# A two-layer decoder trunk: the order of four PSUM banks in the down projection, the PSUM tile of two projection tiles, and the step of two transposes are changed

## The chip, the cores and the metric

The kernel runs on one core of one Trainium2 chip. The metric is the device time of one execution in microseconds (us), lower is better. Three runs of the kernel before took 2271.39, 2271.67 and 2273.57 us, with a median of 2271.67 us.

## The reference

The model has two layers over 1024 tokens of width 1024, in float32. Layer 0 mixes tokens by multi-head latent attention, layer 1 by differential attention (two causal softmax maps per head, whose difference weights the values). After each mixer comes a dense MLP with squared ReLU, and every sub-layer is followed by a residual and a layer norm:

```python
for i in range(2):
    m = mla(x, ...) if i == 0 else diff_attn(x, ...)
    x = layernorm(alpha * x + m)
    x = layernorm(alpha * x + square(relu(x @ w_up)) @ w_down)   # 1024 -> 4096 -> 1024
```

`diff_attn` starts with `x @ w_qkv`, which gives queries, keys and values of 8 heads. The change touches the end of the MLP (the product with `w_down`, the residual and the layer norm) and the first head of `x @ w_qkv` in layer 1.

## The kernel before, in words

All products are made in two float16 halves, so one mathematical product is three matmuls: high by high, high by low, low by high (`mm3`, L186).

**PSUM.** The eight banks are shared by three kinds of tile, two of each: `ps_wide`, 128x1024 float32, which is a pair of banks; `ps_tp`, one bank; `ps_mm`, one bank. The score tiles `ds` of the attention are `ps_wide` tiles, the query/key/value tiles `qkv` are `ps_mm` tiles, and transposes land in `ps_tp`.

**The down projection** (`mixer_out_and_ffn`, once for layer 0 with names ending in A, once for layer 1 ending in B) is done as a fast 2x2 block scheme with seven block products, m = 0 to 6, each summed over NS = 8 steps `st`. A set of four banks, `banks[0..3]`, holds the sums of four token tiles of 128. Sets are taken alternately from two `ps_tp` and two `ps_mm` tiles, and from two `ps_wide` tiles. The last set, that of m = 6, is of `ps_wide` tiles, `w[0]` and `w[1]`: `banks[0]` and `banks[1]` are the halves of `w[0]`, `banks[2]` and `banks[3]` those of `w[1]`. In a step, 24 matmuls write `yA` (or `yB`), six to each bank (`products`). ACT and DVE prepare the operands `h16`, `w16` of the step three later (`d_operands`, L265 and L266). At the end of a set DVE adds the four banks to the rows X2 (`add_y`, L1251).

**The tail.** The last four steps of m = 6 are held back and done bank by bank: for i = 0 to 3, 24 matmuls finish `banks[i]` (called products(i) here), DVE adds it to two rows (add(i)), and the layer norm of row tile 4+i follows: a mean (L1265), a sum of squares on ACT (L1270), a reciprocal root (L160 to L165, over ACT and DVE) and, one i later, the application (L248, L251, called apply(4+i) here) with its store to DRAM on SP's queue.

**The next x.** In layer 0 the finished rows are also transposed for layer 1 (`to_xt`, 8 transposes on PE at L217, two scalings on ACT, two subtractions on DVE). Tiles 0 and 1 are transposed during m = 5, tiles 2 and 3 in the steps (6, 1) and (6, 2), tiles 4 and 5 between the groups of the tail, tiles 6 and 7 after it. On ACT the step (6, 1) and (6, 2) also has squares of the weights of `qkv` (`at`).

**The start of layer 1.** `qkv_part` makes the `qkv` tiles of head 0 for token tiles 0 to 3 first, 24 matmuls each, needing only transposed tiles 0 to 3. Each is then read out by ACT and DVE (`qkv_out`, L1543 to L1546), which frees its PSUM bank. The attention follows, with the later `qkv` tiles as filler between its scores and value products.

**What sets the order.** Inside `with in_order():` each engine keeps the written order. The MLP is one such block, the first four `qkv` tiles are another; between blocks, and in the whole attention, the order on each engine is made when the program is built, by a planner that runs through a simulated timeline (`schedule_with_timeline_sim=True`). On the chip each engine then works through its queue in that order.

Of the kernel before, what the change touches and what calls it, by code (L numbers as in the profile page):

```python
# [72 lines left out]
def trunk(ctx: ExitStack, tc: tile.TileContext, a: dict, inv_freq: bass.AP, out: bass.AP):  # L73
# [16 lines left out]
    def ps_wide(name):  # L90
        return ps.tile([P, 1024], F32, tag="s", name=name)

    def ps_tp(name):
        return ps.tile([P, 512], F32, tag="tp", name=name)

    def ps_mm(name):
        return ps.tile([P, 512], F32, tag="mm", name=name)
# [92 lines left out]
    def p3(lh, ll, rh, rl):  # L190
        return [(lh, rh), (lh, rl), (ll, rh)]
# [16 lines left out]
    def new_xt16(c, nm):  # L208

        return [xtp.tile([P, 2, 4, 512], F16, tag="xt", name=f"xt_{nm}{c}{hf}") for hf in range(2)]  # L210

    def transpose_in16(src, xt_c, ii, nm, scale, tile_of=None):
        for hf in range(2):
            pt = (tile_of or ps_tp)(f"tp_{nm}{hf}")[:, :512].rearrange("p (k q) -> p k q", k=4)
            for k in range(4):
                kk = hf * 4 + k
                nc.tensor.transpose(out=pt[:, k, :], in_=src[:, kk * P : (kk + 1) * P], identity=ident)  # L217
            tk = slice(ii * P, (ii + 1) * P)
            scaled_split(xt_c[hf][:, 0, :, tk], xt_c[hf][:, 1, :, tk], pt, scale)
# [688 lines left out]
    def mixer_out_and_ffn(layer, pa, pb, o_steps, st, n_early, ffn_dst, nm, at={}):  # L908


        with ExitStack() as fs:
# [25 lines left out]
            def up_load(g):  # L937
                raws[g] = tuple(slot(pb, [P, 2, 4, P], F32, f"wu{nm}{g}_r{n}") for n in range(2))
                for f_ in range(2):
                    nc.sync.dma_start(  # L940
                        out=raws[g][f_].rearrange("p z k n -> p (z k) n"), in_=wu[:, :, f_, g, :]
                    )
# [23 lines left out]
            def up_cast(g):  # L966
                raws[g] += (total_in(raws[g][4], f"wu{nm}{g}"),)
# [194 lines left out]
            xt_n = [None, None]  # L1162
# [63 lines left out]
            def bank_set(wide, tag):  # L1226
                if wide:
                    w = [ps_wide(f"y{nm}{tag}{n}") for n in range(2)]
                    return [t[:, hf * 512 : (hf + 1) * 512] for t in w for hf in range(2)]
                return [ps_tp(f"y{nm}{tag}{n}") for n in range(2)] + [ps_mm(f"y{nm}{tag}{n}") for n in range(2)]  # L1230

            def products(dst, i, op, first, last):
# [23 lines left out]
            def to_xt(dst, i, w, tile_of=None):  # L1256
                if i % 4 == 0:
                    dst[i // 4] = new_xt16(i // 4, f"{w}{nm}")
                transpose_in16(X[i], dst[i // 4], i % 4, f"{w}{nm}{i}", sx[:, 2:3], tile_of)
# [33 lines left out]
            for n, i in enumerate(order):  # L1293
# [31 lines left out]
                else:  # L1325
# [4 lines left out]
                    t = x_sums(i - 4, nc.gpsimd if n < NT - 1 else nc.vector)  # L1330
# [10 lines left out]
            with in_order():  # L1341
                for g in range(NG):
                    w = g + 2 < NG
                    if g + 3 < NG:
                        up_load(g + 3)
                    if g + 1 < NG:
                        wd_fetch(g + 1)
                    if w:
                        up_cast(g + 2)
                    if g == NG - 2:  # L1350
                        down_sum(NA, "A")
                    if 0 < g < NG - 1:
                        u_p1(g + 1)
                    u_p7(g)
                    if w:
                        up_scale(g + 2)
                        up_split(g + 2, 0)
                    if g + 1 < NG:
                        u_p6(g + 1)
                    if w:  # L1360
                        up_split(g + 2, 1)
                    if g == NG - 2:
                        down_scale(NA, "A")
                    u_p4(g)
                    if w:
                        up_split(g + 2, 2)
                    if g + 3 < NG:
                        up_sq(g + 3)
                        up_add(g + 3)
                    if g >= NG - 2:  # L1370
                        d_operands(*next(ready))
                    u_p3(g)
                    if w:
                        up_split(g + 2, 3)
                    if g + 1 < NG:
                        if g > 0:
                            u_p2(g + 1)
                        u_p5(g + 1)
                        wd_scan(g + 1)
                    u_out(g)  # L1380
                    if g == NG - 3:
                        for _ in range(3):
                            d_load(*next(loaded))
                d_load(*next(loaded))
                d_operands(*next(ready))

                load_gb("ffn", "f")
                tail, sets = [], 0
                for m, st_ in steps:
                    nxt_ = next(loaded, None)  # L1390
                    if nxt_:
                        d_load(*nxt_)
                    if (m, st_) == (0, 1):
                        for i in range(NT):
                            X[i] = row(f"X2{nm}{i}")
                            nc.sync.dma_start(out=X[i], in_=x2_d[layer, i * P : (i + 1) * P, :])
                    first = st_ == 0 or (m == 0 and st_ == NS - 1)
                    last = st_ == NS - 1 or (m == 0 and st_ == NS - 2)
                    if first:
                        sets += 1  # L1400
                        banks = bank_set(sets % 2 == 0, f"{m}{st_}")
                    late = m == 6 and st_ >= NS - 4
                    if late:
                        tail.append((m, st_))
                    else:
                        for i in range(4):
                            products(banks[i], i, ops[m, st_], first, last)
                        ops.pop((m, st_))
                    if (m, st_) == (0, 0):
                        down_sum(NS, "B")  # L1410
                    if (m, st_) == (0, 2):
                        down_scale(NS, "B")
                    nxt_ = next(ready, None)
                    if nxt_:
                        d_operands(*nxt_)
                    if last and not late:
                        for i in range(4):
                            add_y(banks[i], i, m, "A" if m == 0 and not first else "B")
                    if m == 5:
                        i = st_ // 2  # L1420
                        if st_ % 2 == 0:
                            fin_stats(i)
                        else:
                            if layer == 0 and i in (1, 2):
                                to_xt(xt_n, i - 1, "n", ps_wide)
                            fin_rstd(i)
                            fin_apply(i)
                    if m == 6 and st_ in (1, 2) and layer == 0:
                        to_xt(xt_n, 1 + st_, "n")
                    for step in at.get((m, st_), ()):  # L1430
                        step()
                for i in range(4):
                    for n, key in enumerate(tail):
                        products(banks[i], i, ops[key], False, n == 3)
                    if layer == 0 and i > 1:
                        to_xt(xt_n, 2 + i, "n")
                    add_y(banks[i], i, 6, "B")
                    fin_stats(4 + i)
                    if i > 0:
                        fin_apply(3 + i)  # L1440
                    fin_rstd(4 + i)
                if layer == 0:
                    to_xt(xt_n, 6, "n")
                fin_apply(7)
                if layer == 0:
                    to_xt(xt_n, 7, "n")
# [67 lines left out]
    with ExitStack() as df:  # L1514
# [9 lines left out]
        qkT, dv, dpts, qkv_ps, qk_t, pe1 = {}, {}, {}, {}, {}, {}  # L1524

        def qkv_part(h, i, k0):
            if k0 == 0:
                qkv_ps[h, i] = ps_mm(f"qkv{h}_{i}")[:, :384]
            pq = qkv_ps[h, i]
            for k in (k0, k0 + 1):  # L1530
                xt_ = xt1[i // 4][k // 4]
                xh, xl = (xt_[:, w, k % 4, i % 4 * P : (i % 4 + 1) * P] for w in range(2))
                wh, wl = (w16[h][k // 2][:, w, k % 2 * 384 : (k % 2 + 1) * 384] for w in range(2))
                mm3(pq, p3(xh, xl, wh, wl), first=k == 0, last=k == KT - 1)
            if k0 + 2 == KT:
                qkv_out(h, i, qkv_ps.pop((h, i)))
# [205 lines left out]
```

## Time and profile before

| | |
|---|---|
| median of three runs | 2271.67 us |
| profiled execution, its own time | 2272.7 us |
| its span in the trace | 2270.9 us |
| time around the span | 1.8 us |
| mean granted TensorE clock | 0.972 |
| DVE busy | 1678.9 us (74%) |
| ACT busy | 1279.8 us (56%) |

PE is TensorE's matmuls, PEld its weight loads, DVE VectorE, ACT ScalarE, POOL GpSimd, SP the queue from which the transfers are issued. Times in the trace are from the start of the span. In a timeline a row is a run of like instructions on one engine: start, duration, engine, line, operation, output and inputs, shape and count. A bracket at the end is the time for which the engine sat idle before it, and what ended that. The last granted clock of a window is a share of 2.4 GHz, so 0.50 is 1.2 GHz.

The stages that matter here lie as follows: the down projection of layer 0 from 791.8 us (the first `yA` matmul) to its tail at 1077 to 1128 us, the differential attention after it up to about 1600 us, and the down projection of layer 1 from 1964.1 us to the end.

### The profile page before, as it was taken

How to read it: one execution, taken by the hardware profiler on the slowest of the kernel's cores; microseconds unless marked ns; L12 is line 12 of the kernel's file. 1: busy time of each engine (PE TensorE's matmuls, PEld its weight loads, DVE VectorE, ACT ScalarE, POOL GpSimd, SP SyncE). 2: the span in 40 equal slices, each digit the busy share in tenths (PEclk: the TensorE clock that was granted, in tenths of full speed). 3: DMA queues.
4: the chain of work that ended last, by engine and by line, in shares of the span. 5: the costliest groups of instructions: out<-in, count | busy, mean ns of one | idle time of the engine just before them, and what ended most of it. 6: DMA issues, size and time to landing. Idle time of an engine off the chain costs nothing. (4 is left out here: it accounts for less than half of the span.)

```text
span 2270.9 us, 31756 instructions
## 1 busy us (share of the span) xinstructions
PE 2127.6 (94%) x11255; PEld 1189.7 (52%) x11255; DVE 1678.9 (74%) x2957; ACT 1279.8 (56%) x2384; POOL 488.2 (21%) x363
## 2 busy tenths in 40 slices
PE   7999898989999999998799999978999999999997
PEld 7878775544444444444365666544444444444443
DVE  5577676667777689877677888785667777698787
ACT  5465664446666544447367887774456666444443
POOL 1101000426777410000000000000527776300000
PEclk9999999989999999999899999989999999999999
DMA  5144667526666876665355665454536666966641
GB/s 148 33 99 85 147 128 197 196 89 209 217 214 215 287 288 225 199 197 177 100 98 108 129 125 113 84 127 125 183 122 231 212 219 224 347 224 203 217 150 56
DMA packets 454543, 383.24 MB, mean 169 GB/s; under 512 B 251344, under 2 KB 346592, under 8 KB 454384
## 3 DMA queue, kind: packets, MB, share of 16 engines
q1 hardware_dynamic: 452736, 376.51, 56.0%
q0 software_dynamic: 1648, 4.70, 0.7%
q8 instruction: 88, 1.44, 0.3%
q14 instruction: 71, 0.58, 0.1%
HBM read 246.92 MB, written 83.89 MB: 146 GB/s over the span
## 5 line engine op out<-in xcount | busy, mean ns | idle before, releaser
L186 PE MATMUL yA<-w16A,h16A 128*128 128x512 f16 x1344 | 295.0, 382 | 7.3 <-DVE X2A L1251 3.1
L186 PE MATMUL yB<-w16B,h16B 128*128 128x512 f16 x1344 | 290.9, 379 | 4.6 <-DVE X2B L1251 3.1
L186 PE MATMUL qkv<-wqkv,xt_nA 128*128 128x384 f16 x1536 | 269.4, 330 | 5.5 <-DVE dv L1546 4.5
L186 PEld LDWEIGHTS <-h16A 128*128 128x128 f16 x1344 | 132.2, 98 | 167.7 <-issue 12.8
L186 PEld LDWEIGHTS <-h16B 128*128 128x128 f16 x1344 | 131.3, 98 | 163.9 <-issue 5.8
L186 PEld LDWEIGHTS <-wuA 128*128 128x128 f16 x1344 | 130.8, 98 | 162.1 <-issue 6.9
L186 PEld LDWEIGHTS <-wuB 128*128 128x128 f16 x1344 | 130.4, 98 | 161.8 <-issue 5.9
L186 PEld LDWEIGHTS <-xt_nA 128*128 128x128 f16 x1536 | 150.5, 99 | 102.2 <-issue 11.2
L1614 DVE TENSOR_REDUCE nmx_d<-ds 128x2 f32<-128x256 f32 (+5 forms) x96 | 90.1, 953 | 20.4 <-PE ds L423 19.8
L148 POOL DMA_DIRECT2D lnmgB<-in_ln_mix_g_dram x1 | 0.6, 591 | 467.8 <-PE av_d L186 467.8
L266 DVE SCALAR_TENSOR_TENSOR h16A<-hrA,SCA,h16A 128x1024 f16<-128x1024 f32 x56 | 73.6, 1314 | 36.9 <-ACT h16A L265 36.7
L265 ACT ACTIVATE h16A<-hrA,SCA 128x1024 f16<-128x1024 f32 x56 | 63.8, 1140 | 64.7 <-issue 47.9
L265 ACT ACTIVATE h16B<-hrB,SCB 128x1024 f16<-128x1024 f32 x56 | 63.8, 1140 | 63.8 <-issue 47.9
L266 DVE SCALAR_TENSOR_TENSOR h16B<-hrB,SCB,h16B 128x1024 f16<-128x1024 f32 x56 | 73.7, 1315 | 32.5 <-ACT h16B L265 32.4
L186 PE MATMUL oA<-woA,otA 128*128 128x512 f16 x384 | 87.0, 386 | 4.7 <-DMA otA<-ot_d 4.7
L423 PE MATMUL s<-kn,qn 128*128 128x512 f32 (+2 forms) x288 | 82.9, 383 | 8.1 <-DVE ph L437 7.5
L186 PE MATMUL oB<-woB,otB 128*128 128x512 f16 x384 | 87.6, 385 | 0.0
L266 DVE SCALAR_TENSOR_TENSOR wuA<-wuA_s,cuA,wuA 128x1024 f16<-128x1024 f32 (+1 forms) x32 | 56.4, 1763 | 35.6 <-ACT wuA L265 20.3
L266 DVE SCALAR_TENSOR_TENSOR wuB<-wuB_s,cuB,wuB 128x1024 f16<-128x1024 f32 (+1 forms) x32 | 55.4, 1730 | 35.6 <-ACT wuB L265 20.3
L186 PE MATMUL av_d<-pt16d,dv 128*128 128x256 f16 (+1 forms) x480 | 58.7, 276 | 18.8 <-DMA pt16d<-phd 17.8
L265 ACT ACTIVATE w16B<-wdB,RBB 128x1024 f16<-128x1024 f32 x40 | 45.7, 1142 | 52.4 <-DVE wdB L1208 52.4
L265 ACT ACTIVATE w16A<-wdA,RBA 128x1024 f16<-128x1024 f32 x40 | 45.6, 1141 | 48.2 <-DVE wdA L1208 48.2
(869 smaller groups left out, 5034.3 us busy)
## 6 DMA issues: line engine op xcount, KB each, us to landing
hrA<-hs_d SPq DMA_DIRECT2D x56, 512.0 KB, 4.0
hrB<-hs_d SPq DMA_DIRECT2D x56, 512.0 KB, 3.9
wuA_r<-in_ffn_w_up_dram SPq DMA_DIRECT2D x32, 512.0 KB, 4.4
wdsA<-in_ffn_w_down_dram SPq DMA_DIRECT2D x32, 512.0 KB, 5.0
wdA<-in_ffn_w_down_dram SPq DMA_DIRECT2D x32, 512.0 KB, 4.7
wuB_r<-in_ffn_w_up_dram SPq DMA_DIRECT2D x32, 512.0 KB, 4.2
wdsB<-in_ffn_w_down_dram SPq DMA_DIRECT2D x32, 512.0 KB, 5.0
wdB<-in_ffn_w_down_dram SPq DMA_DIRECT2D x32, 512.0 KB, 4.6
```

Source lines behind the costliest of these rows:

```text
L148: nc.gpsimd.dma_start(out=t, in_=src.to_broadcast([P, n]))
L186: nc.tensor.matmul(dst, l, r, start=first and m == 0, stop=last and m == n - 1, skip_group_check=resumed)
L265: nc.scalar.mul(hi, src, scale)
L266: nc.vector.scalar_tensor_tensor(out=lo, in0=src, scalar=scale, in1=hi, op0=ALU.mult, op1=ALU.subtract)
L423: nc.tensor.matmul(dst, q_, k_(c0 // 512, n), start=m == 0, stop=m == len(pairs) - 1)
L1614: nc.vector.tensor_reduce(out=nmx[:, ms], in_=st["wide"][:, :, :nk] if i < 4 else st[m], axis=AX.X, op=ALU.max, negate=True)
```

## The change

Three edits, none of which changes a number that is computed.

1. `bank_set`: the four banks of a set of two `ps_wide` tiles are dealt out in turn: `banks[0]` and `banks[2]` are now the halves of `w[0]`, `banks[1]` and `banks[3]` those of `w[1]`.
2. `to_xt` of row tiles 2 and 3 of layer 0 is issued in the steps (6, 2) and (6, 3) and no more in (6, 1) and (6, 2).
3. `qkv_part`: the `qkv` tiles of head 0 for token tiles 2 and 3 are the halves of one `ps_wide` tile and no more two `ps_mm` tiles.

```diff
             def bank_set(wide, tag):
                 if wide:
                     w = [ps_wide(f"y{nm}{tag}{n}") for n in range(2)]
-                    return [t[:, hf * 512 : (hf + 1) * 512] for t in w for hf in range(2)]
+                    return [t[:, hf * 512 : (hf + 1) * 512] for hf in range(2) for t in w]
                 return [ps_tp(f"y{nm}{tag}{n}") for n in range(2)] + [ps_mm(f"y{nm}{tag}{n}") for n in range(2)]
...
-                    if m == 6 and st_ in (1, 2) and layer == 0:
-                        to_xt(xt_n, 1 + st_, "n")
+                    if m == 6 and st_ in (2, 3) and layer == 0:
+                        to_xt(xt_n, st_, "n")
...
         def qkv_part(h, i, k0):
-            if k0 == 0:
+            if k0 == 0 and (h, i) == (0, 2):
+                qkv_ps["wide"] = ps_wide("qkv0_2")
+            if k0 == 0 and h == 0 and i in (2, 3):
+                qkv_ps[h, i] = qkv_ps["wide"][:, (i - 2) * 512 : (i - 2) * 512 + 384]
+            elif k0 == 0:
                 qkv_ps[h, i] = ps_mm(f"qkv{h}_{i}")[:, :384]
```

## Rows read from the trace of the kernel before

**Rows 1.** The page, busy time: us (share of span) and count, PE and the others.

```profile
PE 2127.6 (94%) x11255; PEld 1189.7 (52%) x11255; DVE 1678.9 (74%) x2957; ACT 1279.8 (56%) x2384; POOL 488.2 (21%) x363
```

**Rows 2.** Windows: length, busy PE, PEld, DVE, ACT, POOL; then clock, DMA share, GB/s.

```profile
1083.00:1129.00 46.00, 30.09 (x155) 17.05 (x155) 29.40 (x63) 18.64 (x40) 1.54 (x5) 0.85 0.37 115
1086.87:1114.23 27.36, 22.59 (x120) 11.77 (x118) 14.50 (x38) 10.77 (x24) 1.54 (x5) 1.00 0.46 138
1118.00:1130.00 12.00, 5.52 (x22) 4.07 (x23) 7.60 (x16) 4.65 (x11) 0.00 (x0) 0.50 0.21 87
1139.00:1600.00 461.00, 419.02 (x2681) 259.13 (x2680) 353.10 (x824) 331.98 (x813) 6.11 (x6) 0.96 0.56 119
1966.00:2239.00 273.00, 272.17 (x1262) 123.30 (x1262) 228.20 (x246) 126.69 (x129) 10.03 (x6) 1.00 0.58 200
```

**Rows 3.** Timeline of PE, end of layer 0 and start of layer 1.

```profile
1069.00 1.97 PE L217 MATMUL tp_nA<-ident_r,X2A 128*128 128x128 f32 x8 [3.85 <-DVE xt_nA L266]
1070.77 6.95 PE L186 MATMUL yA<-w16A,h16A 128*128 128x512 f16 x24
...
1077.58 5.34 PE L186 MATMUL yA<-w16A,h16A 128*128 128x512 f16 x24
...
1084.22 7.31 PE L186 MATMUL qkv<-wqkv,xt_nA 128*128 128x384 f16 x44 [0.73 <-DVE wqkv L266]
1091.36 10.52 PE L186 MATMUL yA<-w16A,h16A 128*128 128x512 f16 x48
...
1102.21 1.04 PE L217 MATMUL tp_nA<-ident_r,X2A 128*128 128x128 f32 x8
1106.37 5.34 PE L186 MATMUL yA<-w16A,h16A 128*128 128x512 f16 x24 [3.12 <-DVE X2A L1251]
...
1118.56 1.94 PE L217 MATMUL tp_nA<-ident_r,X2A 128*128 128x128 f32 x8 [5.97 <-DVE y_ln_fA L160]
1124.66 1.94 PE L217 MATMUL tp_nA<-ident_r,X2A 128*128 128x128 f32 x8 [4.17 <-DVE X2A L251]
1128.37 9.75 PE L186 MATMUL qkv<-wqkv,xt_nA 128*128 128x384 f16 x48 [1.76 <-DVE dv L1546]
1137.95 0.22 PE L423 MATMUL ds<-qkT 128*128 128x128 f16 x1
```

**Rows 4.** Timeline of DVE and ACT, the same stretch.

```profile
1078.93 1.28 DVE L266 SCALAR_TENSOR_TENSOR h16A<-hrA,SCA,h16A 128x1024 f16<-128x1024 f32 x1 [1.96 <-ACT h16A L265]
...
1086.87 0.75 DVE L1251 SCALAR_TENSOR_TENSOR X2A<-yA,icdBA,X2A 128x512 f32<-128x512 f32 x1
...
1096.74 0.75 DVE L1251 SCALAR_TENSOR_TENSOR X2A<-yA,icdBA,X2A 128x512 f32<-128x512 f32 x1 [5.63 <-PE yA L186]
...
1114.23 0.74 DVE L1251 SCALAR_TENSOR_TENSOR X2A<-yA,icdBA,X2A 128x512 f32<-128x512 f32 x1
...
1126.51 1.60 DVE L266 SCALAR_TENSOR_TENSOR xt_nA<-tp_nA,xs_c,xt_nA 128x512 f16<-128x512 f32 x2 [1.99 <-ACT xt_nA L265]
...
1127.23 0.38 ACT L1543 ACTIVATE qk<-qkv 128x256 f32<-128x256 f32 x1
```

**Rows 5.** Timeline, tail of layer 1, PE and DVE.

```profile
2242.14 10.52 PE L186 MATMUL yB<-w16B,h16B 128*128 128x512 f16 x48 [1.52 <-DVE X2B L1251]
...
2252.81 0.74 DVE L1251 SCALAR_TENSOR_TENSOR X2B<-yB,icdBB,X2B 128x512 f32<-128x512 f32 x1
...
2254.29 5.34 PE L186 MATMUL yB<-w16B,h16B 128*128 128x512 f16 x24 [1.62 <-DVE X2B L1251]
...
2258.01 0.16 DVE L165 TENSOR_TENSOR r_ln_fB<-r_ln_fB,t_ln_fB 128x1 f32<-128x1 f32 x1
...
2259.66 0.75 DVE L1251 SCALAR_TENSOR_TENSOR X2B<-yB,icdBB,X2B 128x512 f32<-128x512 f32 x1 [1.50 <-PE yB L186]
```

**Rows 6.** Waits of PE from 1139 to 1600: total, times, longest, in us.

```profile
PE av_d L186 <- DMA pt16d<-phd: 17.8, 14, 4.2
PE ds L423 <- DVE p_d L1632: 14.8, 4, 7.8
```

## The prediction

> **What bounds the kernel now.** First the page's busy row: PE works 94% of the span and no other engine more than 74% [rows 1], so time is won where PE stands still. The windows say where [rows 2]. In the long down projection of layer 1, PE works 272.17 of 273 us: nothing to win there. At the seam between the layers, 1083 to 1129, it works only 30.09 of 46 us. The attention behind it has 419.02 of 461 us. So I read the seam instruction by instruction.
>
> On PE, four pauses stand out [rows 3]: 3.12 us before the last group of the tail, 5.97 and 4.17 us before the transposes of tiles 6 and 7, 1.76 us before the third `qkv` tile. The reader is to see who ended each. The first was ended by DVE's add of the bank before (L1251). The tail of layer 1 has the same pause twice, 1.52 and 1.62 us [rows 5], and there it sits before products(1) and before products(3), never before products(2): the 48 matmuls from 2242.14 run through from products(1) into products(2), though DVE is then at add(1). Banks 0 and 1 are the halves of one tile, 2 and 3 those of the other. So PE waits only where the bank read last is the other half of the pair that it wants to write. The fourth pause is of another kind: the third `qkv` tile waits until the read-out of the first frees a `ps_mm` bank, and that read-out starts on ACT at 1127.23, after the last transposed tile [rows 4], although its matmuls were long done (44 from 1084.22). ACT and DVE had idle time before; I read it as held there by something that the end of layer 0 sets free, SBUF of its rows most likely. So before 1127 only two `qkv` tiles have a place in PSUM, and PE has nothing to put into its pauses.
>
> **Part 1, banks dealt in turn, layer 1.** products(1) then needs add(0) of no bank in its pair, products(2) comes behind add(0), products(3) behind add(1). A group takes 5.34 us [rows 5], an add of two rows about 1.5 us (0.74 twice), and it is done a group earlier: both pauses go, 1.52 + 1.62 = 3.14 us. What is late next is DVE: its root for tile 6 ended at 2258.01 and add(3) began at 2259.66 [rows 5], a reserve of 1.65 us from the second pause alone. Moving add(1) 1.52 us up moves everything on DVE behind it too, so add(3) could start no earlier than about 2258.1 - 1.5 = 2256.6 by DVE, and 2259.66 - 3.14 = 2256.5 by PE. I take **2.9 us**, all at the end of the kernel, where nothing hides it. Bounds: 0, if the wait is not that of the pair, and 3.14.
>
> The same edit makes add(0) of the inner wide sets ((0,7) to the end of m = 0, m = 2, m = 4) wait for the third group of six matmuls where it now waits for the second: at most 5.34 / 4 = 1.3 us on DVE, six times in both layers, 8 us if all of it came through. Queued behind it on DVE are operands of steps three later. DVE is busy only 228.20 of 273 us there [rows 2] and PE runs steps ahead on stock. I take 0.
>
> **Part 1 in layer 0.** From add(0) at 1086.87 to add(3) at 1114.23 pass 27.36 us [rows 4], in which DVE works 14.50 us [rows 2]. DVE sat 5.63 us before add(1), because products(1), held by the pair, had been planned behind the 44 `qkv` matmuls. Now products(1) can follow products(0) directly, and products(3) need not stand still for 3.12 us. If PE never kept DVE waiting, the idle time left would be the round trips over ACT and PE, some 6 us, so 20.5 us in place of 27.4. That is the upper bound, 6.9 us. The lower is 0, as the two `qkv` tiles must still run somewhere on PE between these links. I take **5 us**, near the upper end, because the row of 5.63 us is a plain hole.
>
> **Part 3, the two `qkv` tiles in a pair.** With a place in PSUM they can run before any read-out: 48 matmuls, which took 9.75 us at the place where they stand, and delayed the first score from 1128.37 to 1137.95, **9.6 us** [rows 3]. PE's free time in 1083 to 1129 is 46 - 30.09 = 15.9 us [rows 2]; 5 + 2 us of it goes as the chain shortens, leaving 8.9. At the full clock the 48 need less: the 44 earlier ones took 7.31 us, 0.166 each, so 8.0 us. It fits, narrowly. The rest of the 9.75 us is clock: 0.50 in 1118 to 1130, after the pauses [rows 2], as also the transposes show (1.94 us for eight, 1.04 at full clock, rows 3). The pair is free once add(2) has read `w[0]`, about the time of products(3); the pauses to be filled come after that. Behind it, the next `qkv` tiles (4, 5) find their `ps_mm` banks free when the first read-outs are done, and cover the way of the first keys to the scores. Bounds: 0 (PE's order has them behind the last transposes) and 9.9.
>
> **Part 2, the transposes of tiles 2 and 3 a step later.** Each moves 8 transposes behind 24 more matmuls on PE, 2 scalings on ACT and 2 subtractions on DVE behind one more pair of operands, and on ACT behind the two squares of the weights; it issues no DMA, and POOL has no part in it. Now PE stops 3.85 us before tile 3, until DVE has subtracted tile 2, and the next 24 matmuls take 6.95 in place of 5.34 us [rows 3]. Afterwards DVE reaches tile 2 at its queue's place behind one more pair of operands, but PE has step (6,2) done by then, and I work out a pause of about 1.2 us, directly ahead of the tail. The last operand pair, for which DVE sat 1.96 us [rows 4], can start when PE has finished (6,3), which it does some 5 us earlier; then DVE's own work is the limit. I take **2 us** for the tail's start. Bounds: -1 (the pause now stands ahead of the tail) and 3.85.
>
> **The sum.** 2.9 + 5 + 9.6 + 2 = 19.5 us. Of the 16.6 won at the seam not all will come through the attention: the order there is planned anew, the filler is used up earlier, and PE already idles 461 - 419.02 = 42 us in it [rows 2]. I charge 2.5 us, an estimate from nothing but that idle time (6% of it). That leaves 17.0: the profiled execution's own 2272.7 becomes 2255.7, and since that execution was 1.0 us above the median of 2271.67, the prediction is **2254.7 us**. With all upper ends (3.1 + 6.9 + 9.9 + 3.9) it is 2247.9.
>
> **Rivals.**
>
> A. The wait is not that of the pair, and the dealing does nothing. For it: the two halves are different banks, and the program could let PE write one while DVE reads the other. The Trainium skill, page "PSUM — Partial Sum Buffer", section "Summary: rules for kernel authors", advises for reading PSUM while a matmul runs to target a different bank, and by that rule products(1) would have had no need to wait for add(0). The trace differs, in that 1.52 and 1.62 us stand at exactly the second half of each pair. Against it: the pause is missing at products(2) in both layers. Then 2.9 and 5 go from the sum: 17.0 - 7.9 = 9.1, 2262.6 us. Chance 0.1.
>
> B. The dealing works, but the two `qkv` tiles stay behind the last transposes in PE's order, or find no room: for it, the narrow fit, and that the planner's timeline, not the chip's, decides; against it, the planner already put the first two tiles into a hole (1084.22). 17.0 - 9.6 = 7.4, 2264.3 us. Chance 0.18.
>
> C. Slower. The attention is planned anew with 9.6 us of filler less. Its place: PE's waits for the transposed weights and for the scores' PSUM, 17.8 and 14.8 us now [rows 6]. `qkv` tiles 2 and 3 also hold one of the two score tiles until they are read out. It decides against the change when PE's 42 us of idle time grow by more than 19.5, by nearly half. At 65 us it would be 2271.7 - 19.5 + 23 = 2275.2. Against it: the waits sit mostly late in the attention, far from the seam. Chance 0.06.
>
> D. The seam and the attention pack better than I charge (all upper ends or beyond): 2248 and less. Chance 0.1.
>
> **How the numbers follow.** My forecast, 2249 to 2260, has 0.56. The range goes from 2246 (most of D) to 2267 (A and B with some loss); C and the far ends are left out. A measurement of this kernel tells about 0.2%, 4.5 us, from no change, so faster means below 2267.1. That holds for the forecast, A, D and most of B: 0.88. Within 0.2%: the rest of B and part of C, 0.08. Slower: 0.04.
>
> **What would show it.** In the profile after: no PE wait on L1251 in either tail, or one well under 0.5 us; `qkv` matmuls, 96 in all, before the transposes of tile 7; no row of 48 at the clock of 0.50; add(0) to add(3) of layer 0 in some 22 us; the first score matmul near 1121 to 1126 and not at 1137.95; PE's wait for xt_nA at about 1 us. The prediction is wrong if PE's idle time between the first score and the end of the attention grows by 8 us or more, or if the pauses before the transposes stay empty.

## The result, and the profile after

The changed kernel takes 2257.21 us (median of four runs, 2255.26 to 2261.14), the kernel before in the same session 2271.53 us. The ratio is 0.9937, with a 95% interval of 0.9925 to 0.9949. So it is faster, by 14.3 us in the medians, and lies inside the predicted range; the median is 2.5 us above the predicted 2254.7. The profiled execution took 2255.26 us (span 2253.4), which is 17.4 less than that of before.

PE's busy time hardly changed, and its share of the span is still 94% [rows 1]:

```profile
PE 2119.3 (94%) x11255; PEld 1185.2 (53%) x11255; DVE 1679.0 (75%) x2957; ACT 1280.0 (57%) x2384; POOL 490.5 (22%) x363
```

The windows of after, with columns as in [rows 2]; the second is add(0) to add(3) of layer 0, which begins and ends earlier now:

```profile
1083.00:1129.00 46.00, 38.91 (x212) 22.17 (x210) 27.28 (x63) 17.35 (x41) 1.77 (x5) 0.93 0.42 123
1083.10:1107.96 24.86, 24.86 (x138) 13.55 (x137) 14.49 (x37) 10.55 (x24) 1.77 (x5) 1.00 0.54 161
1139.00:1600.00 461.00, 419.81 (x2679) 258.26 (x2677) 356.81 (x820) 335.10 (x814) 16.95 (x14) 0.97 0.59 126
1951.00:2225.00 274.00, 272.60 (x1263) 123.39 (x1262) 229.25 (x246) 126.68 (x129) 10.02 (x6) 1.00 0.60 200
```

At the seam PE works 38.91 of 46 us, where it worked 30.09. From add(0) to add(3) it does not stop at all: 24.86 of 24.86 us.

PE's timeline over the seam, to be laid beside [rows 3]:

```profile
1070.66 1.31 PE L217 MATMUL tp_nA<-ident_r,X2A 128*128 128x128 f32 x8 [0.32 <-DVE xt_nA L266]
1075.31 0.16 PE L275 MATMUL tot_wqkv<-totb_wqkv,ones_b 128*128 128x4 bf16 x1 [3.34 <-DVE totb_wqkv L270]
1075.34 12.21 PE L186 MATMUL yA<-w16A,h16A 128*128 128x512 f16 x48
1087.38 1.14 PE L186 MATMUL qkv<-wqkv,xt_nA 128*128 128x384 f16 x6
...
1093.54 1.95 PE L186 MATMUL qkv<-wqkv,xt_nA 128*128 128x384 f16 x11
...
1101.38 4.06 PE L186 MATMUL qkv<-wqkv,xt_nA 128*128 128x384 f16 x24
...
1106.15 5.20 PE L186 MATMUL qkv<-wqkv,xt_nA 128*128 128x384 f16 x31
1112.29 1.06 PE L217 MATMUL tp_nA<-ident_r,X2A 128*128 128x128 f32 x8 [0.94 <-DVE y_ln_fA L160]
1117.75 1.94 PE L217 MATMUL tp_nA<-ident_r,X2A 128*128 128x128 f32 x8 [4.39 <-DVE X2A L251]
1121.44 10.02 PE L186 MATMUL qkv<-wqkv,xt_nA 128*128 128x384 f16 x52 [1.76 <-DVE dv L1550]
1131.30 0.22 PE L423 MATMUL ds<-qkT 128*128 128x128 f16 x1
```

Four things are to be seen. The pauses ended by L1251 are gone: products(0) and products(1) are one run of 48. The pause before the transposes of tile 6 fell from 5.97 to 0.94 us, because 31 `qkv` matmuls stand in it. The one before tile 7 is as long as before, 4.39 us against 4.17. And the 3.85 us before tile 3 became 0.32, but 3.34 us now stand one step later, before the total of the weights' squares (L275).

DVE says why PE stops there, and how the adds lie (beside [rows 4]):

```profile
1073.79 1.40 DVE L266 SCALAR_TENSOR_TENSOR xt_nA<-tp_nA,xs_c,xt_nA 128x512 f16<-128x512 f32 x2
1075.11 0.15 DVE L270 CAST totb_wqkv<-w_sums 128x4 bf16<-128x4 f32 x1
...
1083.10 0.74 DVE L1251 SCALAR_TENSOR_TENSOR X2A<-yA,icdBA,X2A 128x512 f32<-128x512 f32 x1
...
1087.58 0.75 DVE L1251 SCALAR_TENSOR_TENSOR X2A<-yA,icdBA,X2A 128x512 f32<-128x512 f32 x1 [0.24 <-PE yA L186]
...
1098.01 0.74 DVE L1251 SCALAR_TENSOR_TENSOR X2A<-yA,icdBA,X2A 128x512 f32<-128x512 f32 x1
...
1107.96 0.74 DVE L1251 SCALAR_TENSOR_TENSOR X2A<-yA,icdBA,X2A 128x512 f32<-128x512 f32 x1
```

The cast that PE waits for stands in DVE's queue behind the subtractions of tile 3. It stood behind them in the kernel before as well, with an operand pair between:

```profile
1071.91 1.41 DVE L266 SCALAR_TENSOR_TENSOR xt_nA<-tp_nA,xs_c,xt_nA 128x512 f16<-128x512 f32 x2
...
1076.81 0.17 DVE L270 CAST totb_wqkv<-w_sums 128x4 bf16<-128x4 f32 x1
```

Counted from the first `yA`, the cast begins at 285.0 us before and at 284.7 us after, so it did not become later. PE comes to L275 earlier, and waits there for a DVE that has hardly any idle time: DVE works 18.34 of the 19.1 us ahead of add(0) (from 1064 on), where it worked 15.30 of the last 19 us before. The hole of 5.63 us before add(1) is 0.24.

The tail of layer 1, PE and then DVE (beside [rows 5]):

```profile
2225.22 16.78 PE L186 MATMUL yB<-w16B,h16B 128*128 128x512 f16 x77 [0.34 <-DVE w16B L266]
```

```profile
2226.49 0.75 DVE L1251 SCALAR_TENSOR_TENSOR X2B<-yB,icdBB,X2B 128x512 f32<-128x512 f32 x1 [1.33 <-PE yB L186]
...
2231.67 0.75 DVE L1251 SCALAR_TENSOR_TENSOR X2B<-yB,icdBB,X2B 128x512 f32<-128x512 f32 x1 [0.94 <-PE yB L186]
...
2242.15 0.16 DVE L165 TENSOR_TENSOR r_ln_fB<-r_ln_fB,t_ln_fB 128x1 f32<-128x1 f32 x1
2242.23 0.74 DVE L1251 SCALAR_TENSOR_TENSOR X2B<-yB,icdBB,X2B 128x512 f32<-128x512 f32 x1
```

PE runs 77 matmuls without a stop. At add(3) DVE has no idle time ahead: it comes from the root at once, where it had waited 1.50 us for PE. DVE now ends this tail.

The stages of the profiled executions, each from its own landmarks (first `yA`, first score `ds`, first `oB`, first `yB`, last apply), with the number of `qkv` matmuls done before the first score. Only the rows of one execution are compared within a stage; the stretch ahead of the first `yA`, which no edit touches, took between 787.4 and 792.4 us in these executions.

| kernel | down 0 and seam | `qkv` ahead | attention | down 1 and tail |
|---|---|---|---|---|
| before | 346.2 | 96 | 420.1 | 303.1 |
| after | 340.9 | 124 | 413.1 | 300.0 |
| dealing alone | 342.5 | 96 | 421.7 | 300.2 |
| step alone | 344.9 | 96 | 421.1 | 303.1 |
| pair alone | 347.4 | 124 | 413.7 | 303.1 |
| dealing and step | 342.6 | 96 | 419.5 | 300.0 |
| dealing and pair | 346.6 | 124 | 411.6 | 300.1 |
| step and pair | 346.9 | 124 | 413.7 | 303.1 |
| late read-out | 341.5 | 138 | 412.1 | 300.1 |

So the 17.4 us are 5.3 at the seam, 7.0 in the attention, 3.1 in layer 1; of the remaining 2.0, 1.4 lie ahead of the first `yA` and are spread, and the rest is a few tenths in the stages between. The 5.3 and the 7.0 have to be read together: after the change 28 more `qkv` matmuls are done ahead of the first score, and they are missing from the attention's work.

### The profile page after: what moved, and what is told of

It reads as the page before. It is cut to its first block, busy times and chain, and to the rows that moved or that the text cites. A ratio compares the mean times of both kernels' runs of the same rounds, so it can differ in the third digit from the quotient of the medians.

```text
span 2253.4 us, 31757 instructions
## 1 busy us (share of the span) xinstructions
PE 2119.3 (94%) x11255; PEld 1185.2 (53%) x11255; DVE 1679.0 (75%) x2957; ACT 1280.0 (57%) x2384; POOL 490.5 (22%) x363
```

## The experiments

### Which part does what

The three parts one by one, and the kernel after with another place for the last two `qkv` tiles. Each ratio is to the kernel before, run in the same session; the profile is of one execution.

```diff
-                    return [t[:, hf * 512 : (hf + 1) * 512] for t in w for hf in range(2)]
+                    return [t[:, hf * 512 : (hf + 1) * 512] for hf in range(2) for t in w]
```

> The kernel before with the banks dealt in turn and nothing else. Theory (PE waits because the bank read last is the other half of the tile it writes): the PE waits on L1251 vanish in both tails, 3.1 us at the end of the kernel; in layer 0 add(0) to add(3) takes about 25 us in place of 27.4; the third and fourth qkv tiles stay at the seam. In all 4.5 to 6 us less than before, about 2266 us. Rival (the pauses come from something else, as DVE's lag): the pauses stay, no change of time beyond 1.5 us.

Measured: 2266.31 us, ratio 0.9981 (0.9971 to 0.9991). Both pauses on L1251 are gone in both layers, add(0) to add(3) takes 22.79 us, and layer 1 gives 2.9. PE's timeline, the end of the seam:

```profile
1104.04 1.04 PE L217 MATMUL tp_nA<-ident_r,X2A 128*128 128x128 f32 x8
1111.05 1.94 PE L217 MATMUL tp_nA<-ident_r,X2A 128*128 128x128 f32 x8 [5.98 <-DVE y_ln_fA L160]
...
1120.86 10.42 PE L186 MATMUL qkv<-wqkv,xt_nA 128*128 128x384 f16 x48 [1.76 <-DVE dv L1546]
```

The dealing shortens the chain to the last transposed tile, and leaves the pause before tile 6 and the 48 slow matmuls: those are another matter. Of the 4.6 us won in the chain, 3.6 show at the first score, and 1.6 of them are missing again at the end of the attention.

```diff
-                    if m == 6 and st_ in (1, 2) and layer == 0:
-                        to_xt(xt_n, 1 + st_, "n")
+                    if m == 6 and st_ in (2, 3) and layer == 0:
+                        to_xt(xt_n, st_, "n")
```

> The kernel before with only the transposes of tiles 2 and 3 a step later. Theory: the pause of 3.85 us before tile 3 shrinks below 1.5 us, add(0) of layer 0 starts about 3 us earlier (1084 in place of 1086.9), and as everything behind it is the same, 2 to 3 us less than before, about 2269 us. Rival (the gain is eaten by the pause that now stands ahead of the tail, or by the 44 qkv matmuls behind products(0)): less than 1 us.

Measured: 2277.19 us, ratio 1.0016 (1.0004 to 1.0027): no gain, rather slower, where 2 to 3 us less were expected. The profiled execution was one of the quicker ones (2269.9 us). PE's timeline:

```profile
1070.45 1.32 PE L217 MATMUL tp_nA<-ident_r,X2A 128*128 128x128 f32 x8 [0.32 <-DVE xt_nA L266]
1075.09 0.16 PE L275 MATMUL tot_wqkv<-totb_wqkv,ones_b 128*128 128x4 bf16 x1 [3.33 <-DVE totb_wqkv L270]
1075.12 6.86 PE L186 MATMUL yA<-w16A,h16A 128*128 128x512 f16 x24
```

The pause moved with its price: 3.85 us before, and 24 matmuls in 6.95 us behind it [rows 3]; here 0.32 + 3.33 us, and 24 matmuls in 6.86. The tail does start sooner, add(0) at 292.3 us after the first `yA` in place of 295.1, but add(3) only by 1.0 us and the first score by 1.2.

```diff
-            if k0 == 0:
+            if k0 == 0 and (h, i) == (0, 2):
+                qkv_ps["wide"] = ps_wide("qkv0_2")
+            if k0 == 0 and h == 0 and i in (2, 3):
+                qkv_ps[h, i] = qkv_ps["wide"][:, (i - 2) * 512 : (i - 2) * 512 + 384]
+            elif k0 == 0:
                 qkv_ps[h, i] = ps_mm(f"qkv{h}_{i}")[:, :384]
```

> The kernel before with only the third and fourth qkv tiles in one pair of banks. Theory (a write to one half waits until the other half has been read, here too): only the third tile runs before the transposes of tile 7, 72 qkv matmuls in all and not 96; the fourth comes after the third's read-out. Half of the 9.6 us: 4 to 6 us less than before, about 2266.5 us. Rival (both tiles fit before the read-outs, as the prediction had it): 96 matmuls before the transposes of tile 7 and 9 to 10 us less, about 2262 us.

Measured: 2268.49 us, ratio 0.9987 (0.9977 to 0.9997), 3.0 us less in the medians and so short of the expected 4 to 6. PE's timeline:

```profile
1116.58 1.94 PE L217 MATMUL tp_nA<-ident_r,X2A 128*128 128x128 f32 x8 [5.98 <-DVE y_ln_fA L160]
...
1126.39 10.61 PE L186 MATMUL qkv<-wqkv,xt_nA 128*128 128x384 f16 x52 [1.76 <-DVE dv L1550]
```

Here, too, 72 of the `qkv` matmuls of tiles 0 to 3 stand ahead of the last transposes, not 96, and none of them in the pause before tile 6. The 52 behind it are the other half of the pair, 24, and 28 of the next tiles.

```diff
-            if k0 == 0 and (h, i) == (0, 2):
-                qkv_ps["wide"] = ps_wide("qkv0_2")
             if k0 == 0 and h == 0 and i in (2, 3):
-                qkv_ps[h, i] = qkv_ps["wide"][:, (i - 2) * 512 : (i - 2) * 512 + 384]
+                qkv_ps[h, i] = ps_wide(f"qkv{h}_{i}")[:, :384]
```

> The changed kernel, but the third and fourth qkv tiles have a pair of banks each and use its first half. Theory (what held the fourth tile back was the other half of its pair): all 96 qkv matmuls run before the transposes of tile 7, the pause of 4.39 us there shrinks below 2 us, and the kernel takes 2 to 5 us less than the changed one, that is 16.5 to 19.5 us less than before, about 2253.5 us. Rival (the fourth tile is held by something that the end of layer 0 frees, as its read-out is): the order and the time stay those of the changed kernel within 1 us. A second rival: both pairs of banks are then taken and the first scores wait for them, 1 to 4 us more than the changed kernel.

Measured: 2254.67 us, ratio 0.9926 (0.9914 to 0.9939). With a pair of its own for each tile all 96 matmuls run ahead of the transposes of tile 7, 55 of them in one run. So it was the shared pair that held the fourth tile back. The pause before tile 7, which I expected to shrink, stayed at 4.39 us, and the ratio's interval overlaps that of the change, so a gain in time is not shown.

### The parts in twos, and the read-out

The three pairs are made of the diffs above: parts 1 and 2, parts 1 and 3, parts 2 and 3.

> The changed kernel without the pair of banks for the third and fourth qkv tiles (parts 1 and 2 alone). The single parts moved the median by -5.2 (banks dealt), +5.7 (step later) and -3.0 us (pair), the whole by -14.3. Theory (PE's pauses at the seam are one hole that the parts close together: the first two move the links, only the pair fills what is left): the pauses of about 4 and 6 us before the last transposes stay, 4 to 8 us less than before, about 2265.5 us. Rival (the parts add up): about 2272 us, no change.

Measured: 2263.12 us, ratio 0.9956 (0.9940 to 0.9972): 10.6 us less in the medians, more than the expected 4 to 8. The pauses stayed, 4.84 and 4.17 us.

> The changed kernel without the later step of the two transposes (parts 1 and 3). Theory (part 2 gains some 2.4 us at the start of the tail, as the traces show): 9 to 12 us less than before, about 2261 us, that is 3 to 4 us more than the changed kernel. Rival (part 2 by itself brings a new pause of 3.3 us before the total of the weights' squares and gains nothing): the time of the changed kernel or less, 2254 to 2257 us.

Measured: 2258.66 us, ratio 0.9934 (0.9918 to 0.9950): the rival came, not the theory.

> The changed kernel without the dealing of the banks (parts 2 and 3). Theory: the pauses on L1251 are back (3.1 us in each tail, products(1) again behind 34 qkv matmuls), 72 qkv matmuls before the transposes of tile 7 but the pause before tile 6 stays about 6 us; 3 to 7 us less than before, about 2266.5 us. Rival (parts add up, -3.0 and +5.7): 2274 us.

Measured: 2266.57 us, ratio 0.9973 (0.9961 to 0.9985).

Parts 1 and 3 without part 2 give what all three give (0.9934 against 0.9937). In the medians they also give more together than apart: 6.6 per thousand against 1.9 and 1.3. A likely place is the pause before tile 6: alone, neither the dealing nor the pair fills it (5.98 us in both); together it is 4.03, and in the kernel after 0.94. But the stages of the table, summed, hardly show it: 4.9 us for the dealing, 5.2 for the pair, 11.0 for both. So the reason for the excess is not shown. Part 2 changes sign with its company, +1.6 per thousand alone, -1.4 beside the pair and -2.5 beside the dealing; in the whole it gives nothing that these runs can tell.

The kernel after, in which the read-out of tile 2 is written behind the matmuls of tile 3:

```diff
             if k0 + 2 == KT:
+                if (h, i) == (0, 2):
+                    return
+                if (h, i) == (0, 3):
+                    qkv_out(0, 2, qkv_ps.pop((0, 2)))
                 qkv_out(h, i, qkv_ps.pop((h, i)))
```

> The changed kernel, with the read-out of the third qkv tile written behind the matmuls of the fourth; the pair of banks is as in the changed kernel. Theory (the fourth tile's matmuls wait for the read-out of the third because it reads the other half of their pair, and for nothing else): all 96 qkv matmuls run before the transposes of tile 7 though the tile is the same pair, and the time is that of the kernel with a pair for each, 1 to 4 us less than the changed kernel, about 2254.7 us. Rival (two pairs were needed for another reason, as the scores' place): the order and time of the changed kernel, about 2257 us.

Measured: 2253.47 us, ratio 0.9910 (0.9894 to 0.9925). PE's timeline:

```profile
1103.79 9.10 PE L186 MATMUL qkv<-wqkv,xt_nA 128*128 128x384 f16 x55
1112.73 1.04 PE L217 MATMUL tp_nA<-ident_r,X2A 128*128 128x128 f32 x8
...
1121.61 8.77 PE L186 MATMUL qkv<-wqkv,xt_nA 128*128 128x384 f16 x42 [1.76 <-DVE dv L1554]
```

The tiles still share a pair; only the order of reading and writing is another, and all 96 matmuls run early. This shows it most directly: a matmul into one half waits for the read of the other half, if that read is written ahead of it. In the kernel after, tile 3 was written behind the read-out of tile 2, and so fell behind the last transposes.

### The pair wait in the tail

The kernel before, with the banks in the order first half of `w[0]`, first of `w[1]`, second of `w[1]`, second of `w[0]`:

```diff
-                    return [t[:, hf * 512 : (hf + 1) * 512] for t in w for hf in range(2)]
+                    return [w[n][:, hf * 512 : (hf + 1) * 512] for n, hf in ((0, 0), (1, 0), (1, 1), (0, 1))]
```

> The kernel before, with the four banks of a wide set taken in a third order: first half of w[0], first of w[1], second of w[1], second of w[0]. Theory (PE waits for the read of the other half of the pair that it wants to write): in the tail of layer 1 one pause on L1251 of about 1.5 us, before products(2), and none before products(1) or products(3), where the kernel before has one before each of these. Rival (the wait is for the bank finished last, whichever it is): a pause before each group, or where they stood.

One execution, 2269.8 us. The tail of layer 1, PE:

```profile
2246.12 10.52 PE L186 MATMUL yB<-w16B,h16B 128*128 128x512 f16 x48 [1.52 <-DVE X2B L1251]
```

and DVE's adds:

```profile
2239.45 0.75 DVE L1251 SCALAR_TENSOR_TENSOR X2B<-yB,icdBB,X2B 128x512 f32<-128x512 f32 x1 [1.33 <-PE yB L186]
...
2244.64 0.75 DVE L1251 SCALAR_TENSOR_TENSOR X2B<-yB,icdBB,X2B 128x512 f32<-128x512 f32 x1 [0.93 <-PE yB L186]
...
2251.50 0.75 DVE L1251 SCALAR_TENSOR_TENSOR X2B<-yB,icdBB,X2B 128x512 f32<-128x512 f32 x1 [1.50 <-PE yB L186]
...
2256.78 0.74 DVE L1251 SCALAR_TENSOR_TENSOR X2B<-yB,icdBB,X2B 128x512 f32<-128x512 f32 x1
```

Now there is one pause, and it stands before products(2), where neither kernel had one: the adds lie 5.19, 6.86 and 5.28 us apart. Four banks in another order, and the wait goes exactly where the bank just read is the other half of the pair. So rival A's ground falls. The Trainium skill, page "PSUM — Partial Sum Buffer", section "Summary: rules for kernel authors", advises another bank for reading beside a matmul; here another bank did not spare the wait, PE stood 1.52 us until the read of the other half. The wait is one for a semaphore of DVE's add, so it shows the order that the program keeps by tile; whether PE and DVE could work on the two banks of a pair at once, no run here tests.

The tail is 1.7 us shorter than before (17.33 against 19.00 us), yet down projection and tail together took 303.0 us as before: add(0) comes 1.6 us later after the first `yB`. In this order the other half of bank 0's pair is the bank that a step writes last. DVE now waits 2.9 us in all before the first adds of two inner sets, where it did not wait before, and PE waits 1.60 us for `w16B` ahead of the tail, where it waited 0.20, most of it in one place:

```profile
2228.61 9.22 PE L186 MATMUL yB<-w16B,h16B 128*128 128x512 f16 x42 [1.26 <-DVE w16B L266]
```

So the price for the inner sets, which the prediction took at 0 for its own order, exists, and a worse order pays it.

### What is left of the pauses

The late read-out, with the cast of the weights' squares a step earlier, ahead of the subtractions of tile 3:

```diff
-    at[6, 2] = [lambda n=n: qkv_sq(0, n) for n in range(2, 4)]
-    at[6, 3] = [lambda: qkv_cast(0)]
+    at[6, 2] = [lambda n=n: qkv_sq(0, n) for n in range(2, 4)] + [lambda: qkv_cast(0)]
```

> The kernel with the late read-out (all three parts, all 96 qkv matmuls early), and the cast of the sums of the qkv weights one step earlier on DVE, in (6, 2). Theory (part 2 gained nothing since it put that cast behind the subtractions of tile 3, and PE stood 3.3 us before the total): that pause falls below 0.5 us, and 2 to 4 us less than the kernel with the late read-out, 2250.5 us at before's 2273.7. Rival (DVE sets the start of the adds in any case, and PE's pause was free): the same time within 1 us.

Measured: 2252.44 us, ratio 0.9914 (0.9899 to 0.9928), the same as without it. PE's timeline:

```profile
1072.23 0.17 PE L275 MATMUL tot_wqkv<-totb_wqkv,ones_b 128*128 128x4 bf16 x1
1072.26 4.26 PE L186 MATMUL yA<-w16A,h16A 128*128 128x512 f16 x19
1078.04 6.42 PE L186 MATMUL yA<-w16A,h16A 128*128 128x512 f16 x29 [1.53 <-DVE w16A L266]
```

The pause of 3.33 us is gone, as expected; 1.53 us before the next operand took part of its place. But the adds did not start sooner: add(0) begins 292.4 us after the first `yA`, 292.1 without the early cast. That is what the rival said: DVE, idle for no more than 0.8 us in the 18 us ahead of add(0) in either, sets that start, and for it PE's pause was free. The first score comes 3.9 us sooner after the first `yA` (337.6 against 341.5) with 7 `qkv` matmuls fewer done; in the time of the whole nothing of it can be told.

The late read-out without part 2 (transposes of tiles 2 and 3 back in the steps (6, 1) and (6, 2)):

```diff
-                    if m == 6 and st_ in (2, 3) and layer == 0:
-                        to_xt(xt_n, st_, "n")
+                    if m == 6 and st_ in (1, 2) and layer == 0:
+                        to_xt(xt_n, 1 + st_, "n")
```

> The kernel with the late read-out but without part 2 (transposes of tiles 2 and 3 in the old steps). Theory (part 2 is worth nothing net): within 2 us of the kernel with the late read-out, ratio to the kernel before near 0.991. Rival (part 2 is worth the 2 to 3 us by which the start of the tail is earlier in the traces): ratio 0.992 to 0.9925.

Measured: 2252.27 us, ratio 0.9911 (0.9896 to 0.9926). Again part 2 can be left out at no cost that shows.

The early cast, with the matmuls of `qkv` tile 3 held behind the transposes of tile 6 in PE's order, so that they fill the pause before tile 7:

```diff
+                    behind["pe"] = next(i for i in reversed(nc.cur_bb.bb.instructions) if i.engine == nc.tensor.engine)
...
+            if (h, i, k0) == (0, 3, 0):
+                tc.add_manual_dep(
+                    next(x for x in traced[begin:] if x.engine == nc.tensor.engine),
+                    behind["pe"].name,
+                    mybir.DependencyInfo(mybir.DependencyClass.NoSync, mybir.DependencyReason.DATA),
+                    reason="in_order",
+                )
```

> The kernel with the cast early, and the fourth qkv tile held on PE behind the transposes of tile 6, so that its 24 matmuls stand in the pause of 4.4 us before the transposes of tile 7. Theory (with all 55 before tile 6, its transposes come about 2 us late and the pause before tile 7 stays at 4.4 us): that pause falls below 1 us, no clock of one half behind it, and 1.5 to 4 us less than the kernel with the cast early. Rival (what ends last is DVE's chain from the adds to the last subtraction, not PE): the same time within 1 us.

Measured: 2259.46 us, ratio 0.9942 (0.9929 to 0.9954): 7.0 us slower in the medians than without the hold, where 1.5 to 4 us less were expected. PE's timeline, and a window and a wait from its attention:

```profile
1113.08 1.94 PE L217 MATMUL tp_nA<-ident_r,X2A 128*128 128x128 f32 x8 [4.19 <-DVE y_ln_fA L160]
1114.82 5.61 PE L186 MATMUL qkv<-wqkv,xt_nA 128*128 128x384 f16 x24
1120.27 1.04 PE L217 MATMUL tp_nA<-ident_r,X2A 128*128 128x128 f32 x8
```

```profile
1233.00:1283.00 50.00, 44.86 (x286) 28.19 (x284) 37.54 (x92) 35.18 (x94) 0.00 (x0) 0.93 0.57 121
```

```profile
PE av_d L186 <- DMA pt16d<-phd: 26.4, 12, 5.1
```

The pause before tile 7 is gone, and the one before tile 6 is back: 24 matmuls fill one of two pauses of over 4 us, and the other opens. At the first score that is a draw (2.2 us later after the first `yA`, with 13 more `qkv` matmuls done, some 2.1 us by the late read-out's 55 in 9.10). Most of the loss is in the attention, 417.7 us against 412.9 for the early cast: its order was planned anew, its wait for the transposed weights is 26.4 us against 23.2, and one window of 50 us in it runs at a granted clock of 0.93 and the next at 0.97, where the early cast has 1.00 throughout that stretch. Why the planner's new order is the worse one was not settled.

## Why the prediction was right, and which of its steps were not

The sign, the size and the cause of most of it were right: 17.0 us predicted for the profiled execution, 17.4 measured, 14.3 in the medians. But the terms are not the predicted ones. The seam was to give 16.6 us and gave 5.3, the attention was to cost 2.5 and gave 7.0, and some 2 us of the 17.4 belong to stages that no edit touches. That the sum for the profiled execution came out within half a microsecond is in good part luck.

**Dealing, layer 1** (2.9): right. The stage lost 3.1 us; in every execution with the dealing it lasts 300.0 to 300.6 us, in every one without it 303.0 to 303.1. The reserve on DVE was sized rightly too: add(3) now follows its root without a gap.

**Inner sets** (0): right to a few tenths. DVE waits 0.17 us before the first add of two inner sets in layer 1, PE waits 0.34 us for an operand ahead of the tail in place of 0.20, and add(0) comes 0.2 us later after the first `yB` (276.8 against 276.6).

**Dealing, layer 0** (5): right by itself, and in part booked twice in the sum. Alone it took 4.6 us out of the chain (27.36 to 22.79). With the pair beside it the chain is 25.06 us: PE is busy for all of that time, and 24 `qkv` matmuls stand ahead of the transposes of tile 5 where 12 stood, which cost the chain some 2 us that they save later. The sum counted the shorter chain and the free filling both. The 24.86 us of the whole are no clean measure of this, since the step lengthens the chain too (25.56 with dealing and step, without the pair): add(0) comes sooner by it, add(3) hardly.

**Pair** (9.6): the step that failed is "with a place in PSUM they can run before any read-out". For tile 2 it held. Tile 3 is the other half of the pair, and waited for the read-out of tile 2 by the very rule on which part 1 rests. So 72 matmuls, not 96, ran ahead of tile 7, and 52 stood behind it, at a granted clock of 0.50 just before them (1117.7 to 1121.5) and of 0.86 over them. The first score came at 1131.30 and not at 1121 to 1126.

A second step failed, that these matmuls delayed the first score by their whole 9.6 us. In the kernel before, the first keys are on their way for most of that time:

```profile
1131.15 1.48 SPq L1572 DMA_TRANSPOSE qkT<-dz  x1
```

That transfer took 3.7 us from issue to landing. So the first score could have come at about 1134.9 (an estimate from these two), 3.1 us ahead of 1137.95, without the 48 matmuls. With all 96 early (late read-out) it came 341.5 us after the first `yA`, with 42 matmuls of the next tiles ahead of it, against 346.2 before. What the filling saves has to be won in the attention, and that is where the gain came:

```profile
1138.00:1558.00 420.00, 251.50 (x1441) 17.02 (x61) 33.87 (x122) 0.96 0.55 113
```

```profile
1131.30:1544.40 413.10, 244.13 (x1413) 16.53 (x60) 33.47 (x120) 0.96 0.57 115
```

These are the windows of the attention (first score to first `oB`), before and after, with the `qkv` instructions alone (length, PE, DVE, ACT, clock, DMA share, GB/s). 28 matmuls fewer were left for it, 7.4 us of PE's time, and it became 7.0 us shorter. With the pair added to the dealing, the medians' ratio went from 0.9981 to 0.9934, some 11 us: about what the term had promised, by another way, since the first score came 4.1 us later (346.6 against 342.5 us after the first `yA`) and the attention became 10.1 us shorter. The two profiled executions differ by only 6.1 us, so the size is loose. What held the first read-outs behind the last transposed tile, SBUF by the prediction's reading, was not tested.

**Attention charge** (-2.5): not seen. PE's idle time in it stayed (420.1 - 378.12 = 42.0 us before, 413.1 - 371.91 = 41.2 after). Rival C's place got 2.5 us worse in all, far from the 19.5 that it needed:

```profile
PE av_d L186 <- DMA pt16d<-phd: 19.8, 16, 4.1
PE ds L423 <- DVE p_d L1636: 15.3, 4, 8.4
```

against 17.8 and 14.8 us [rows 6]. That time can be lost there is shown by the held tile 3: 4.8 of its 7.0 us, with the first of these waits at 26.4 us.

**The step of two transposes** (2): right at the start of the tail, and worth nothing that shows in the time of the whole. The pause before tile 3 went as predicted, even further (0.32 us, about 1.2 worked out), DVE lost its idle time as worked out, and add(0) came 2.4 us sooner after the first `yA` (292.7 against 295.1). What failed is that PE's time would come free with it: PE stands 3.34 us for the cast before L275, which the prediction does not name, since DVE comes to that cast no earlier than before. And the earlier add(0) does not show at the end: beside the two other parts the time without part 2 is the same within the intervals (0.9934 against 0.9937; with the late read-out 0.9911 against 0.9910).

Of the rivals, A is out (the order of four banks), B came half true (one tile of two stayed behind), C and D did not come. Of the signs that the prediction named against itself, one came by half: the pause before tile 6 was filled, the one before tile 7 stayed empty.

What stays open: the pieces of the profiled executions and the medians disagree by up to some 4 us where part 2 is in or out, so a gain of 1 or 2 us by it is not excluded. The best versions (late read-out, with or without part 2 or the early cast) are at 0.9910 to 0.9914; their intervals reach that of the change, so a gain of some 5 or 6 us on top of it is likely and not proven.

## What to carry to other kernels

When a tile spans two banks, order its writes and reads as if it were one: a write to one half stands behind a read of the other half, if that read is written first. When a pause is closed by moving work, ask whether the engine that was waited for has idle time left: if it has none, the pause moves to the next thing that it delivers, as from tile 3 to the cast. And do not book both a shorter chain and free filling between its links: PE has that time once.

## What the runs showed of the hardware

Executions of one kernel differ by 2 to 15 us (the kernel before from 2264.68 to 2279.20 over all sessions), in part with the mean granted clock: the four of the changed kernel took 2255.26 and 2255.54 us at 0.979, 2258.88 and 2261.14 at 0.974 and 0.975. The twelve of the step alone went from 2268.99 us at 0.975 to 2279.77 at 0.969. So two profiles alone do not decide 5 us.

A pause at PE can cost more than its length. Behind 3.34 us of idling 48 matmuls took 12.21 us, at a granted clock of 0.86, where 48 without a pause took 10.52 [rows 3]; eight transposes behind 4.39 us took 1.94 us, at 0.50, behind 0.94 us 1.06. It need not: in the kernel before, 24 matmuls behind 3.12 us took 5.34 us at a clock of 1.00, as without a pause [rows 3].
